# Attention as one pipeline of 48 head pairs, with two modulation units moved from VectorE to TensorE

## The chip, the cores and the metric

The kernel runs on one core of one Trainium2 chip. The metric is the device time of the whole program in microseconds (us); a comparison takes the medians of runs that alternate on the same chip.

## The reference, cut to what matters

Two layers of a diffusion backbone run over 512 latent tokens and 256 context tokens, with 1024 features. Every layer first turns a conditioning vector into six modulation vectors (shift, scale and gate for the mixer, shift, scale and gate for the feed-forward network), once for the latent stream and once for the context stream. Layer 0 mixes tokens by attention, layer 1 by retention; each is followed by a gated feed-forward network.

```python
mx = split(silu(c) @ ada_w[i] + ada_b[i], 6)          # latent; mc is the same with c_ctx
h_x = rms_norm(x, norm1_g) * (1 + mx[1]) + mx[0]
# layer 0: 16 heads of 64, 4 key/value heads, blocks of 128 queries; q and k are normalised, q_x and k_x rotated
s = [q @ k_ctx, q @ k_window (masked outside |i-j| <= 128), sink]   # context queries: k_ctx and sink alone
p = softmax(s);  o = p[:, ctx] @ v_ctx + p[:, window] @ v_window
x = x + mx[2] * (o @ w_o)
x = x + mx[5] * swiglu(rms_norm(x, norm2_g) * (1 + mx[4]) + mx[3])
```

The change concerns layer 0 alone, from the attention blocks to the start of its feed-forward network.

## The kernel before, in words

Activations are kept transposed, features on the 128 partitions and tokens along the free axis. A float32 product is made of three products of rounded parts (`mm3`, L145-151): high times high, low times high, high times low. Weights arrive as 512 KB chunks on SyncE's DMA queue (`w_raw`, L121); ScalarE rounds a chunk to its high part and VectorE subtracts to get the low part (`next_w`, L137).

**Order of work.** Apart from short stretches that are fixed by hand, a list scheduler places the instructions of every engine when the program is built. It goes by the order in which the Python code issues them, by when it thinks that operands are ready, and by which tile buffers are free. Each engine then runs its own list strictly in order, and waits at an instruction until the semaphores it needs have come.

**One block.** `Block` (L650) holds one group of four query heads, one stream and one block of 128 queries. There are 4 groups with 4 latent and 2 context blocks each, so 24 blocks, or 48 pairs of heads. For each head `score` (L660) issues the score products on TensorE into one of three PSUM banks (`S`, L685) and the masked minimum on VectorE (L686, a custom instruction that also stores the scores as the tile `pr`). After each second head it issues ScalarE's exponentials with row sums (L102, called through `lnexp`), VectorE's reciprocal (L696) and GpSimd's scaling of the two heads' probabilities (L699). `pr` has 8 buffers, so four pairs. `turn` (L701) transposes four 128x128 pieces of probabilities on TensorE into one of two PSUM banks `pT` (L705), and ScalarE or VectorE copies the bank to a tile `tt` (L709). `output` (L725) multiplies values by the transposed probabilities (L732) into `pO`.

**The loop.** `attend` (L749) takes one block after the other: the four heads' scores, then an optional filling piece, then all transposes of the block, then its output. After blocks 1 and 3 of groups 0 to 2 all four pieces of the next query tile's projection (`make_q`, L548) are issued in a row, between two blocks. During group 3 parts of the output projection (`out_part`, L833) are the filling pieces.

**Modulation.** In layer 0 the shift and the scale for the feed-forward network (parts 3 and 4 of `mods`) come from two places. Features 0 to 511 are made on TensorE before attention, in units of four feature tiles (`ada_unit`, L303; `UNITS` on L28 names the units made there, of which 8 and 6 are these). Features 512 to 1023 are made on VectorE during the rest of the output projection: `ada_tile` (L264) loads a 512 KB transposed tile on SyncE's queue and makes two multiply-and-sum instructions (L272), one for each stream; `cond_rows` (L256) loads the two conditioning vectors, spread over all partitions, and ScalarE applies the silu to them. `WO_ADA` (L30) says after which output tile how many of the eight tiles are issued.

**After attention.** The remaining output tiles follow in `WO_ORDER`. Each ends in a gated addition (L254), a square on ScalarE (L208 or L210) and an addition to the sum of squares (L211). After the tile (1, 4) the latent norm is closed (`rms`, L218 and L197 to L199). `latent_shape` (L909) then makes the eight operands of the feed-forward network, each by a scaling (L914), a rounding (L915) and a subtraction (L916), and `first_two` uses them one feature tile at a time.

Of the kernel before, what the change touches and what calls it, by code (L numbers as in the profile page):

```python
# [14 lines left out]
P = 128  # L15
# [6 lines left out]
NKV = 4  # L22
# [7 lines left out]
WO_ADA = {(0, 3): 1, (0, 4): 2, (0, 5): 2, (0, 6): 2, (0, 7): 1}  # L30
SPLIT_AT = (2, 4)
# [19 lines left out]
def dit_kernel(ctx, tc, xT, cT, crow, small, consts, masks, tabs0, tabs1, jtab, adaQ, adaN, adaT, wst, out):  # L51
# [132 lines left out]
    def t_sq(n):  # L184
        return T(rp, 512, "sq", 2)[:, :n]
# [464 lines left out]
    class Block:  # L650
# [9 lines left out]
        def score(self, i):  # L660
# [19 lines left out]
            for c0, w, m0, parts in runs:  # L680
                bank = pS()[:, :w]
                for p0, pw, kk in parts:
                    for r in range(2):
                        keys = kk[g][r] if kk is kc else kk[g][r][:, x0:x0 + pw]
                        nc.tensor.matmul(bank[:, p0:p0 + pw], qt, keys, start=r == 0, stop=r == 1)  # L685
                nc.vector.tensor_tensor_reduce(pt[:, c0:c0 + w], bank, mask[:, m0:m0 + w], 1.0, top, add, ALU.min, lo)  # L686
                top = lo
# [13 lines left out]
        def turn(self, kis, heads, eng):  # L701

            tp = pT()
            for i, (ki, hd) in enumerate((ki, hd) for ki in kis for hd in heads):
                nc.tensor.transpose(tp[:, i * P:(i + 1) * P], self.pr[hd][:, ki * P:(ki + 1) * P], ident)  # L705
# [3 lines left out]
            self.last = nc.scalar.copy(dst, tp) if eng == 0 else nc.vector.tensor_copy(dst, tp)  # L709
# [38 lines left out]

    def attend(g, s, b, *fills):  # L749
        blk = Block(g, s, b)  # L750
        for i in range(4):
            blk.score(i)
        for f in fills[:1]:
            f()
        blk.turns()
        for f in fills[1:]:
            f()
        blk.output()
# [57 lines left out]
    streams = ((0, xr), (1, cres))  # L816
# [13 lines left out]
    wo = [cut(next_w(ap, 1)), cut(next_w(ap, 1)), key_room_w(), cut(next_w(ap, 1))]  # L830
    begun = {}
# [13 lines left out]
    early = [(0, 0, 0, 3), (0, 0, 3, 6), (1, 0, 0, KT), (1, 1, 0, KT), (1, 2, 0, KT), (0, 1, 0, 6)]  # L845
    for (s, b), part in zip(context + latent, early):
        fills = [lambda: out_part(*part)]
        if (s, b) == latent[-1]:
            fills.append(lambda: out_part(1, 3, 0, KT, pS))
        attend(NKV - 1, s, b, *fills)  # L850
# [22 lines left out]
    assert not ada_wo  # L873
# [965 lines left out]
```

## Time and profile before

| | |
|---|---|
| median of 3 runs | 1772.69 us (1772.52 to 1777.53) |
| the profiled execution, whole | 1774.28 us |
| its span, first to last instruction | 1772.5 us |
| granted TensorE clock, mean | 0.995 |
| TensorE busy | 1716.1 us |
| VectorE, ScalarE, GpSimd busy | 1351.8, 845.4, 125.9 us |

Times in the profile are counted from the first instruction. The attention blocks run from about 104 to 331 us, the rest of the output projection from there to about 380 us, and the feed-forward network of layer 0 follows. PE is TensorE, PEld its weight loads, which run beside its products; DVE is VectorE, ACT ScalarE, POOL GpSimd, SP SyncE. An idle time is put down to the instruction whose end released the waiting one. A product is drawn longer than the interval at which the next one can start, so the busy time of PE hides short gaps.

### The profile page before, as it was taken

The page shows a single profiled execution, that of the slowest core. Times are in us where ns is not written, and L with a number is a line of the kernel's source. Part 1 is how long each engine was busy: PE and PEld are TensorE (multiplying, and loading weights), DVE is VectorE, ACT ScalarE, POOL GpSimd, SP SyncE. Part 2 cuts the span into 40 slices and gives each one's busy share as a digit, 9 for nine tenths or more (in the row PEclk, how much of TensorE's full clock was granted, in tenths as well). Part 3 has the DMA queues.
Part 4 walks back from the last instruction along what each step waited for, and adds up shares of the span by engine and source line. Part 5 has one row for each costly group of instructions (what it writes and reads, how often), then busy time and mean ns, then how long its engine had stood idle before and what let it go on. Part 6 is the DMA issues. An engine that isn't in the chain of part 4 may idle for free.

```text
span 1772.5 us, 27621 instructions
## 1 busy us (share of the span) xinstructions
PE 1716.1 (97%) x10852; PEld 1528.1 (86%) x10852; DVE 1351.8 (76%) x2366; ACT 845.4 (48%) x1486; POOL 125.9 (7%) x267
## 2 busy tenths in 40 slices
PE   6899999999999999999998999999999999999999
PEld 4787777779999999999977888898897899999998
DVE  6687777598778788777799858758768798777774
ACT  5476677455333334342465534524525564445442
POOL 0024334100000000000010000000000000000000
PEclk9999999999999999999999999999999999999999
DMA  8601012334243434343343434434433323233222
GB/s 337 238 25 37 25 43 66 118 123 152 83 144 119 156 107 154 112 152 110 116 133 104 160 97 140 151 102 132 155 96 119 95 77 116 94 109 107 96 84 84
DMA packets 59890, 206.68 MB, mean 117 GB/s; under 512 B 6640, under 2 KB 7024, under 8 KB 59504
## 3 DMA queue, kind: packets, MB, share of 16 engines
q1 hardware_dynamic: 52848, 179.75, 30.8%
q0 software_dynamic: 6912, 25.17, 4.5%
q8 instruction: 85, 1.39, 0.3%
q14 instruction: 45, 0.37, 0.1%
HBM read 202.80 MB, written 2.10 MB: 116 GB/s over the span
## 4 chain that ended last, share of the span: by engine, by line
PE 75%; DVE 14%; DMA 4%; ACT 3%; issue 2%; POOL 2%; SPq 0%; DVEq 0%; ACTq 0%; POOLq 0%
PE Y L883 14%; PE Z L883 7%; PE pj L149 6%; PE pj L151 6%; PE pj L150 6%; PE X L883 3%; PE Z L1241 3%; PE Y L1228 3%; DMA wraw<-in_wst_dram 3%; DVE wlo L167 3%; PE pT L705 2%; PE pO L732 2%; PE pj L1241 1%; PE X L1228 1%; POOL pr L699 1%
## 5 line engine op out<-in xcount | busy, mean ns | idle before, releaser
L166 ACT CAST whi<-wraw 128x1024 fp32r<-128x1024 f32 x177 | 185.8, 1053 | 307.2 <-PE Z L151 71.5
L167 DVE TENSOR_TENSOR wlo<-wraw,whi 128x1024 fp32r<-128x1024 f32 x177 | 216.0, 1223 | 42.3 <-ACT whi L166 41.9
L883 PE MATMUL Y<-aq,whi 128*128 128x384 f32 x640 | 173.5, 335 | 0.7 <-ACT hn L1021 0.7
L254 DVE SCALAR_TENSOR_TENSOR res<-pj,mod,res 128x512 f32<-128x512 f32 (+1 forms) x110 | 80.4, 731 | 68.4 <-PE pj L151 67.4
L142 DVE TENSOR_TENSOR wlo<-wraw,whi 128x1024 fp32r<-128x1024 f32 x79 | 96.5, 1223 | 35.3 <-ACT whi L141 34.3
L141 ACT CAST whi<-wraw 128x1024 fp32r<-128x1024 f32 x79 | 82.9, 1051 | 74.1 <-PE Z L151 24.2
L883 PEld LDWEIGHTS Y<-aq,whi 128*128 128x128 f32 x640 | 116.6, 188 | 1.7 <-ACT hn L1021 1.2
L883 PE MATMUL Y<-aq,wlo 128*128 128x384 f32 x320 | 107.0, 334 | 0.0
L272 DVE CUSTOM_DVE_ANT_0 y<-adaw,crow,small_sb 128x1024 bf16<-128x1024 f32 x64 | 81.9, 1280 | 31.6 <-DMA adaw<-in_adaT_dram 31.4
L102 ACT ACTIVATE pr<-pr,stat,qs 128x513 f32<-128x513 f32 (+2 forms) x96 | 74.4, 779 | 16.7 <-DVE stat L692 16.6
L1241 PE MATMUL Z<-whi,sA 128*128 128x512 f32 x256 | 81.0, 392 | 0.7 <-ACT whi L166 0.7
L699 POOL TENSOR_SCALAR pr<-pr,stat 128x512 f32<-128x512 f32 (+2 forms) x96 | 69.1, 733 | 90.6 <-DVE stat L696 86.4
L149 PE MATMUL pj<-ax,whi 128*128 128x512 f32 x176 | 68.7, 391 | 0.0
L151 PE MATMUL pj<-ax,whi 128*128 128x512 f32 x176 | 68.7, 390 | 0.0
L150 PE MATMUL pj<-ax,wlo 128*128 128x512 f32 x176 | 68.5, 389 | 0.0
L705 PE MATMUL pT<-const_sb,pr 128*128 128x128 f32 x352 | 58.0, 283 | 9.8 <-POOL pr L699 7.8
L149 PE MATMUL pj<-act,whi 128*128 128x512 f32 x168 | 66.0, 393 | 0.0
L150 PE MATMUL pj<-act,wlo 128*128 128x512 f32 x168 | 65.9, 392 | 0.0
L151 PE MATMUL pj<-act,whi 128*128 128x512 f32 x168 | 65.5, 390 | 0.0
L705 PEld LDWEIGHTS pT<-const_sb,pr 128*128 128x128 f32 x352 | 39.3, 140 | 27.9 <-POOL pr L699 21.0
L269 POOL DMA_DIRECT2D adaw<-in_adaT_dram x48 | 25.7, 535 | 516.9 <-DVE mod L272 419.8
L686 DVE CUSTOM_DVE_ANT_0 pr<-S,mask,qs 128x256 f32<-128x256 f32 (+1 forms) x96 | 52.6, 566 | 10.9 <-PE S L685 9.2
(539 smaller groups left out, 5275.2 us busy)
## 6 DMA issues: line engine op xcount, KB each, us to landing
wraw<-in_wst_dram SPq DMA_DIRECT2D x238, 512.0 KB, 3.7
adaw<-in_adaT_dram POOLq DMA_DIRECT2D x48, 512.0 KB, 3.9
wx<-in_wst_dram SPq DMA_DIRECT2D x24, 512.0 KB, 4.7
adan<-in_adaQ_dram SPq DMA_DIRECT2D x16, 512.0 KB, 7.8
adan<-in_adaN_dram SPq DMA_DIRECT2D x16, 512.0 KB, 8.8
res<-in_xT_dram SPq DMA_DIRECT2D x16, 256.0 KB, 4.2
adaw<-in_adaT_dram SPq DMA_DIRECT2D x8, 512.0 KB, 4.0
aq<-in_adaN_dram SPq DMA_DIRECT2D x12, 256.0 KB, 5.6
```

The costliest lines, as they stand in the source:

```text
L141: nc.scalar.copy(hi, raw)
L142: nc.vector.tensor_tensor(lo, raw, hi, op=sub)
L149: nc.tensor.matmul(o, whi, xhi, start=first, stop=False)
L150: nc.tensor.matmul(o, wlo, xhi, start=False, stop=False)
L151: return nc.tensor.matmul(o, whi, xlo, start=False, stop=last)
L166: nc.scalar.copy(hi, t)
L167: return nc.vector.tensor_tensor(lo, t, hi, op=sub)
L272: after(nc.vector.tensor_tensor_reduce(junk, w, cr[:, s * 1024:(s + 1) * 1024], 1.0, sm_t[:, C_ADAB + l * 48 + j:C_ADAB + l * 48 + j + 1], ...
L699: nc.gpsimd.tensor_scalar(pt[:, :n], pt[:, :n], st[:, 6 + e:7 + e], 1.0, op0=mult, op1=mult)
L705: nc.tensor.transpose(tp[:, i * P:(i + 1) * P], self.pr[hd][:, ki * P:(ki + 1) * P], ident)
L883: nc.tensor.matmul(o, p, r, start=first and k + i == 0, stop=k == 3 and i == 2, skip_group_check=not first)
L1241: ins = nc.tensor.matmul(o, p, r, start=first and k + i == 0, stop=k == 3 and i == 2, skip_group_check=not first)
```

## The change

1. `attend` is gone. One loop runs over the 48 head pairs. In step `i` it issues the scores of pair `i`, then the transposes of pair `i - 2` (`LAG`), then filling pieces listed by step number (`steps`), then the output of a block whose second pair has been transposed. The first transpose in a step is ordered behind the last score product of the step's first head (`behind`).
2. The four pieces of each query projection are issued in different steps.
3. The eight feature tiles of parts 3 and 4 no longer run on VectorE. Units 7 and 9 make them on TensorE in group 3, each in two halves over the contraction (`unit_half`): four loads of 256 KB into buffers of the query tiles, 16 small products, a copy by ScalarE, a transpose, two small additions by VectorE. `cond_rows`, the eight 512 KB loads and the 16 VectorE instructions before the feed-forward network go.
4. Splitting of outputs, stream loads and output weights are placed at steps too.

What follows the output projection is not changed; it stands 25 lines further down.

```diff
-WO_ADA = {(0, 3): 1, (0, 4): 2, (0, 5): 2, (0, 6): 2, (0, 7): 1}
-SPLIT_AT = (2, 4)
+LAG = 2
...
-        def turn(self, kis, heads, eng):
+        def turn(self, kis, heads, eng, behind=()):
...
+                if i == 0:
+                    after(ins, behind)
...
-        def turns(self):
+        def turns(self, p, behind):
             n = len(self.keys)
-            for p in range(2):
-                for ki in range(0, n - 1, 2):
-                    self.turn((ki, ki + 1), (2 * p, 2 * p + 1), ki // 2 % 2)
-            if n % 2:
+            for ki in range(0, n - 1, 2):
+                self.turn((ki, ki + 1), (2 * p, 2 * p + 1), ki // 2 % 2, () if ki else behind)
+            if p and n % 2:
                 self.turn((n - 1,), (0, 1, 2, 3), 0)
...
-    for g in range(NKV - 1):
-        for i, (s, b) in enumerate(latent + context):
-            attend(g, s, b)
-            if i in (1, 3):
-                for piece in make_q(2 * g + 2 + i // 3):
-                    piece()
-            if (g, i) == SPLIT_AT:
-                split_o(0)
-                split_o(1)
-    split_o(2)
-    xr = load_stream(0)
-    cres = load_stream(1)
...
-    early = [(0, 0, 0, 3), (0, 0, 3, 6), (1, 0, 0, KT), (1, 1, 0, KT), (1, 2, 0, KT), (0, 1, 0, 6)]
-    for (s, b), part in zip(context + latent, early):
-        fills = [lambda: out_part(*part)]
...
-        attend(NKV - 1, s, b, *fills)
+    def unit_half(u, c):
+
+        part, o, w = u // 2, pT()[:, 0:P], []
+        for k in range(4 * c, 4 * c + 4):
+            w.append(T(ap, 512, "q", 9))
+            nc.sync.dma_start(w[-1], adaN[u, k // 2][:, k % 2 * 512:k % 2 * 512 + 512])
+        for k in range(4):
+            for j in range(4):
+                nc.tensor.matmul(o[32 * j:32 * j + 32, :], ccol[:, 4 * c + k, :], w[k][:, j * P:(j + 1) * P],
+                                 start=k == 0, stop=k == 3)
+        rows = t_sq(P)
+        nc.scalar.copy(rows, o)
+
+        def finish():
+            t = pT()[:, 0:P]
+            nc.tensor.transpose(t, rows, ident)
+            tv = t.rearrange("p (j c) -> p c j", c=32)
+            for s in range(2):
+                col = mods[0, s][:, part, 4:8]
+                nc.vector.tensor_tensor(col, tv[:, s, :], col if c else sm_t[:, C_ADAB + 4 * u:C_ADAB + 4 * u + 4], op=add)
...
+    for g in range(NKV - 1):
+        a, b = make_q(2 * g + 2), make_q(2 * g + 3)
+        for r, fs in ((0, a[0:1]), (2, a[1:2]), (3, a[2:4]), (5, b[0:1]), (8, b[1:2]), (9, b[2:3]), (10, b[3:4])):
+            steps[12 * g + r] = list(fs)
+    steps[34].append(lambda: split_o(0))
+    steps[35] = [lambda: split_o(1), weight]
+    last = {1: [lambda: unit_half(7, 0)], 2: [lambda: split_o(2), load_streams, lambda: out_part(0, 0, 0, 4), end],
+            3: [lambda: unit_half(7, 1), weight], 4: [lambda: out_part(0, 0, 4, 6), end],
+            5: [lambda: unit_half(9, 0), lambda: weight(key_room_w)], 6: [end, lambda: out_part(1, 0, 0, KT)],
+            7: [lambda: unit_half(9, 1), weight], 8: [end, lambda: out_part(1, 1, 0, KT)],
+            10: [lambda: out_part(1, 2, 0, KT)], 11: [lambda: out_part(0, 1, 0, 3)],
+            12: [lambda: out_part(0, 1, 3, 6)], 13: [lambda: out_part(1, 3, 0, KT, pS)]}
+    steps.update({12 * (NKV - 1) + r: fs for r, fs in last.items()})
+    blocks = [Block(g, s, b) for g in range(NKV) for s, b in (latent + context if g < NKV - 1 else context + latent)]
+    for i in range(2 * len(blocks) + LAG):
+        behind = ()
+        if i < 2 * len(blocks):
+            blk = blocks[i // 2]
+            blk.score(i % 2 * 2)
+            behind = [blk.scored]
+            blk.score(i % 2 * 2 + 1)
+        j = i - LAG
+        if j >= 0:
+            blk = blocks[j // 2]
+            blk.turns(j % 2, behind)
+        for f in steps.get(i, ()):
+            f()
+        if j >= 0 and j % 2:
+            blk.output()
...
-    ada_wo = [(part, d) for part in (3, 4) for d in range(4, KT)]
...
-    cr = cond_rows(wo_p)
+    (_, xr), (_, cres) = streams
     for s, d in WO_ORDER:
-        ins = out_part(s, d, 0, KT)
-        for _ in range(WO_ADA.get((s, d), 0)):
-            ada_tile(0, *ada_wo.pop(0), (0, 1), cr, [ins], wo_p)
+        out_part(s, d, 0, KT)
         if (s, d) == (1, 4):
             ln_exp_turn()
             rms(0)
```

More of the change, by code (lines that the diff above doesn't have):

```diff
@@ L684, in score @@
                         keys = kk[g][r] if kk is kc else kk[g][r][:, x0:x0 + pw]
-                        nc.tensor.matmul(bank[:, p0:p0 + pw], qt, keys, start=r == 0, stop=r == 1)
+                        self.scored = nc.tensor.matmul(bank[:, p0:p0 + pw], qt, keys, start=r == 0, stop=r == 1)
                 nc.vector.tensor_tensor_reduce(pt[:, c0:c0 + w], bank, mask[:, m0:m0 + w], 1.0, top, add, ALU.min, lo)
@@ L699, in score @@
                 nc.gpsimd.tensor_scalar(pt[:, :n], pt[:, :n], st[:, 6 + e:7 + e], 1.0, op0=mult, op1=mult)
-        def turn(self, kis, heads, eng):
+        def turn(self, kis, heads, eng, behind=()):
             tp = pT()
             for i, (ki, hd) in enumerate((ki, hd) for ki in kis for hd in heads):
-                nc.tensor.transpose(tp[:, i * P:(i + 1) * P], self.pr[hd][:, ki * P:(ki + 1) * P], ident)
+                ins = nc.tensor.transpose(tp[:, i * P:(i + 1) * P], self.pr[hd][:, ki * P:(ki + 1) * P], ident)
+                if i == 0:
+                    after(ins, behind)
             while len(self.tt) <= kis[0] // 2:
@@ L747, in output @@
             nc.vector.tensor_copy(dst, O.rearrange("p (e q) -> p e q", e=2))
[L749 to L758, printed above, removed]
     def split_o(g):
@@ L803, in dit_kernel, with load_streams @@
     latent, context = ([(s, b) for b in range(n)] for s, n in ((0, 4), (1, 2)))
[L804 to L816 removed]
+    streams = []
+    def load_streams():
+        streams.extend(((0, load_stream(0)), (1, load_stream(1))))
     def cut(w):
@@ L843, in out_part @@
         return ins
-    early = [(0, 0, 0, 3), (0, 0, 3, 6), (1, 0, 0, KT), (1, 1, 0, KT), (1, 2, 0, KT), (0, 1, 0, 6)]
-    for (s, b), part in zip(context + latent, early):
-        fills = [lambda: out_part(*part)]
-        if (s, b) == latent[-1]:
-            fills.append(lambda: out_part(1, 3, 0, KT, pS))
-        attend(NKV - 1, s, b, *fills)
+    def unit_half(u, c):
[16 more added lines that the diff above has]
+                nc.vector.tensor_tensor(col, tv[:, s, :], col if c else sm_t[:, C_ADAB + 4 * u:C_ADAB + 4 * u + 4], op=add)
+        ends.append(finish)
@@ new lines, in dit_kernel @@
+    ends = []
+    end = lambda: ends.pop(0)()
+    weight = lambda room=None: wo.append(room() if room else cut(next_w(ap, 1)))
+    steps = {}
+    for g in range(NKV - 1):
[10 more added lines that the diff above has]
+            12: [lambda: out_part(0, 1, 3, 6)], 13: [lambda: out_part(1, 3, 0, KT, pS)]}
@@ L872, in dit_kernel @@
             rms(0)
-    assert not ada_wo
     A.close()
```

3 lines of the change are left out of this document (1 added, 2 removed).

## The prediction

> **What bounds the kernel now.** I read the page first: the busy times, and the chain that ended last.
>
> ```profile
> span 1772.5 us, 27621 instructions
> ...
> PE 1716.1 (97%) x10852; PEld 1528.1 (86%) x10852; DVE 1351.8 (76%) x2366; ACT 845.4 (48%) x1486; POOL 125.9 (7%) x267
> ...
> PE 75%; DVE 14%; DMA 4%; ACT 3%; issue 2%; POOL 2%; SPq 0%; DVEq 0%; ACTq 0%; POOLq 0%
> ```
>
> TensorE is the bound, so what the change is worth is what it takes out of TensorE's waits, less what it adds to TensorE's work. Next come the windows of the two stages that it touches: attention, and the change-over from the output projection to the feed-forward network.
>
> ```profile
> core 0: us, PE busy (x) PEld busy (x) DVE busy (x) ACT busy (x) POOL busy (x), PEclk, DMA share, GB/s
> 103.80:330.70 226.90, 216.85 (x1519) 172.06 (x1518) 169.41 (x546) 154.87 (x368) 86.38 (x190) 1.00 0.11 34
> ...
> 369.00:380.00 11.00, 10.18 (x78) 8.96 (x77) 11.00 (x22) 4.80 (x9) 0.00 (x0) 1.00 0.18 48
> 380.00:390.00 10.00, 6.82 (x27) 4.17 (x27) 10.00 (x18) 9.93 (x18) 0.00 (x0) 1.00 0.28 106
> 390.00:420.00 30.00, 30.00 (x204) 29.70 (x206) 27.49 (x51) 19.52 (x39) 0.39 (x1) 1.00 0.55 188
> ```
>
> In attention PE seems 96% busy and VectorE is at 169.41 of 226.90 us, 75%: no helper is full. From 369 to 390 VectorE is busy without a pause, and PE lacks 0.82 + 3.18 = 4.0 us. After 390 PE is full, and in the built order of the changed kernel all that follows the change-over stands as before (8070 TensorE instructions, unbroken to the end). So a microsecond won before 390 is won at the end. The granted clock (PEclk) is 1.00 throughout and gives nothing.
>
> A product is drawn longer than its interval, so I look at the weight loads' waits in the attention window for the true gaps, and at one gap in the timeline.
>
> ```profile
> PEld pT L705 <- POOL pr L699: 21.0, 48, 1.3
> PEld S L685 <- DVE stat L686: 2.3, 8, 0.5
> PEld pO L732 <- ACT tt L709: 1.8, 6, 0.5
> ```
> ```profile
> 143.82 0.30 PE L705 MATMUL pT<-const_sb,pr 128*128 128x128 f32 x1
> 144.88 0.33 PE L705 MATMUL pT<-const_sb,pr 128*128 128x128 f32 x1 [0.77 <-POOL pr L699]
> ```
>
> Transposes wait 48 times, 21.0 us together, for GpSimd's scaled probabilities; all else is small. This is what the lag aims at.
>
> **The lag.** How long does TensorE have between the last score product of a pair and its first transpose, and how long do the probabilities take? The first comes from the built orders of both kernels, counting the products that stand between, each at its interval.
>
> ```profile
> 344.70 0.39 PE L150 MATMUL pj<-h,wlo 128*128 128x512 f32 x1
> 344.93 0.39 PE L151 MATMUL pj<-h,whi 128*128 128x512 f32 x1
> ...
> 297.40 1.95 PE L732 MATMUL pO<-tt,v 128*64 128x256 f32 x16
> ...
> 301.51 1.04 PE L705 MATMUL pT<-const_sb,pr 128*128 128x128 f32 x8
> ```
>
> 512 columns start 0.23 us apart, so 384 and 256 columns cost 0.17 and 0.115; eight transposes take 1.04 us, of which the last is drawn at 0.28, so 0.11 each; a value product is 0.11 likewise. On this scale the 48 pairs of the kernel before have a median of 5.0 us of TensorE work between their last score and their first transpose. In the changed order it is 7.0 us. For the second number I follow the last two pairs from their score products to GpSimd:
>
> ```profile
> 313.19 0.40 PE L685 MATMUL S<-k,q 128*128 128x256 f32 x2
> ...
> 316.74 0.49 PE L685 MATMUL S<-k,q 128*128 128x256 f32 x2
> ```
> ```profile
> 319.56 1.36 POOL L699 TENSOR_SCALAR pr<-pr,stat 128x512 f32<-128x512 f32 x2 [4.51 <-DVE stat L696]
> 321.16 1.37 POOL L699 TENSOR_SCALAR pr<-pr,stat 128x512 f32<-128x512 f32 x2 [0.24 <-DVE stat L696]
> ```
>
> Scores end at 313.59, the first head is scaled at 319.56 + 0.68 = 320.24: 6.6 us. For the other pair, 317.23 to 321.85: 4.6 us. Summing over the pairs what is missing to such a time: at 4.6 us the old order lacks 8.2 us and the new one 1.1; at 6.6 us the old lacks 63.7 and the new 23.4. The measured wait of 21.0 lies between, since one wait also gives the pairs behind it their time. A time of 5.2 us reproduces it (old 20.8), and then the new order lacks 4.4. Scaling the 6.6 us case to the measured wait instead, 23.4 x 21.0 / 63.7 = 7.7 remain. I take 7, near the less favourable end, because the helpers' same work then falls into less time. **The lag brings 21.0 - 7 = 14 us**, with bounds of 0 (the chain gets as much later as the transposes do) and 21.
>
> The query pieces are the same instructions, spread; they cost nothing themselves and are part of the counted distances. With lag 2, three pairs of `pr` are live and there is room for four, so GpSimd's small copies into a new `pr` need not wait for transposes of a pair that is late; were they to wait, the scaling queued behind them on GpSimd would wait as well, which is within the bound of 0.
>
> **Off VectorE.** Sixteen instructions leave the output projection.
>
> ```profile
> L272 DVE CUSTOM_DVE_ANT_0 junk<-adaw,crow,small_sb x16: 1273/1278/1286, 348.3 to 373.9; 128x1024 bf16<-128x1024 f32 x16
> ```
> ```profile
> 375.05 0.69 DVE L199 SCALAR_TENSOR_TENSOR y<-sq,y 128x512 f32<-128x512 f32 x1
> ...
> 378.07 0.74 DVE L914 SCALAR_TENSOR_TENSOR act<-res,acol,y 128x512 f32<-128x512 f32 x1
> ```
> ```profile
> 371.75 0.64 ACT L197 ACTIVATE sq<-y 128x512 f32<-128x512 f32 x1
> ```
> ```profile
> 380.86 0.44 PE L149 MATMUL Y<-aq,whi 128*128 128x384 f32 x1 [0.72 <-ACT whi L141]
> ...
> 384.26 0.44 PE L149 MATMUL X<-aq,whi 128*128 128x384 f32 x1 [0.69 <-ACT aq L915]
> ```
>
> They are 16 x 1.28 = 20.5 us of VectorE, but not of the path: from 331 to 369 PE runs on. What they delay is the norm. ScalarE has its square at 372.39, VectorE finishes the norm only at 375.74 and starts the first operand at 378.07. Without them I count from 372.4: the two steps of the norm, L198 and L199, at 0.69 each give 373.8; what the changed order puts between them and the first operand (a gated addition and sums of squares, half as wide) may take as much again, 375.2. So the first operand starts 3 to 4 us sooner. PE lacks 4.0 us there, and the chain of eight operands behind the first is as long as before, with context squares and a weight split between its links, so some of the waits on ScalarE and VectorE stay. I take **3 us**, with 1 and 4 as bounds. The weights move up past eight 512 KB loads and the 1 MB row on SyncE's queue; PE did not wait for them there, so that earns nothing.
>
> **On to TensorE.** Units 7 and 9 add 64 small products and 4 transposes.
>
> ```profile
> L309 PE MATMUL pj<-aq,ccol x96: 272/273/297, 419.1 to 421.6; 128*32 128x128 f32 x96
> ```
>
> 2.5 us for 95 steps are 0.026 us each, so 64 x 0.026 + 4 x 0.11 = 2.1 us, and about 1 us for going to and fro between other products: **3 us**. ScalarE's four copies and VectorE's eight small additions are no more than what fills their idle quarter. The loads are the less certain part.
>
> ```profile
> aq<-in_adaN_dram SPq DMA_DIRECT2D x12, 256.0 KB, 5.6
> ...
> crow<-in_adaN_dram SPq DMA_DIRECT2D x4, 256.0 KB, 4.1
> ```
>
> Their buffers come from the nine of the query tiles, of which six are live in group 3. So the fourth load of the first half waits on SyncE until TensorE has read a context query for the last time; behind it in the queue stand stream loads that wait for `split_o(2)`, then the next half's loads, then output weights. Between that release and the product that needs the fourth load, the order has 3.3 us of TensorE work; a group of four takes 4.1 us to land, so about 0.8 is missing. I put 0.5 on each of four halves: **2 us**, with 0 and 4 x 5.6 = 22 as bounds. A half also keeps one of the two `pT` banks; that is in the 2.
>
> The Trainium skill's "DMA: Bandwidth & Descriptors" (Anatomy of one DMA) gives a load a fixed cost of about 2.0 us plus its bytes at 436 GB/s, so a 256 KB load would be an estimated 2.6 us, and the fourth load would then arrive before it is needed. The rows of this trace, 4.1 and 5.6 us for loads issued in groups, do not agree with that as a price here; by the page the sum would be 2 us lower.
>
> **The sum.** -14 - 3 + 3 + 2 = -12 us, against the profiled execution's 1774.28 (span 1772.5 and 1.8 around it): 1762.3. The median of the runs, 1772.69, is 1.6 below the profiled time, so I forecast 1772.7 - 12 = **1760.7 us**.
>
> **Rivals.**
> (a) The chain is the limit, not its start: probabilities come later as the transposes do, because VectorE, ScalarE and GpSimd work their own lists in order. Then the lag brings perhaps 4 us and the sum is -4 - 3 + 3 + 2 = -2: **1770.7**. For it: ends of 6.6 us above bare work. Against it: VectorE at 75%, ScalarE at 154.87 of 226.90.
> (b) Loads of the unit halves come late, slower than before: TensorE's list is in order, so each half can hold it for a whole landing, 4 x 5.6 = 22.4 us. -14 - 3 + 3 + 22.4 = +8.4: **1781**. It turns the sign once a half costs over 14 / 4 = 3.5 us. For it: the queue behind `split_o(2)` and the buffers released late. Against it: 3.3 us of work ahead of the first of them, and DMA at 11% in this window. At the page's 2.6 us a half, this rival would end at about 1769, no slower than before.
> (c) All waits go, in both stages: -21 - 4 + 3 + 0 = -22: **1750.7**.
> (d) The scheduler undoes the order, so nothing moves: **1772.7**. The built order speaks against it (5.0 against 7.0 us).
>
> **How the numbers follow.** Forecast 0.62, its own range 1753 to 1768; (a) 0.14; (b) 0.10; (c) 0.10; (d) 0.04. A difference under 0.3% (5.3 us) can't be told from none. Faster: 0.61 of the forecast, (c), and 0.03 of (a): 0.74. Same: the rest of (a), (d) and the forecast: 0.16. Slower: 0.10. The range from (c) to just beyond (a) and (d), 1750 to 1774, leaves out (b) and the far end of (c), about 0.2 at most.
>
> **What would show it.** Right: the wait of the transposes for L698 (now L699) near 7 us; the first operand (L939) 3 us sooner after the norm's square, with PE's idle time there down to about 1 us; waits of PE for `adaN` loads in group 3 near 2 us. Wrong: transposes waiting 15 us or more although they stand later (a); one of the unit products waiting 3 us and more for a load (b); or new waits of scores for their bank (2.3 us now) or of value products for copies (1.8 us now) that take the place of the old one.

## The result, and the profile after

The changed kernel takes 1767.7 us against 1773.0 for the one before, medians of nine alternating runs each. The ratio of their means is 0.9967 (95% interval 0.9956 to 0.9977), so 5.9 us faster (4.1 to 7.8); the medians alone differ by 5.3. The forecast was 12 us. The direction held, and half of the gain is missing.

The page of the changed kernel (its profiled execution took 1765.14 us, the one of before 1774.28, so this pair is 9.1 us apart, more than the means):

```profile
span 1763.4 us, 27889 instructions
...
PE 1716.5 (97%) x10984; PEld 1531.5 (87%) x10984; DVE 1332.7 (76%) x2342; ACT 841.3 (48%) x1487; POOL 122.4 (7%) x267
```

The windows of the same stages as in the prediction (length, busy time of TensorE, its weight loads, VectorE, ScalarE and GpSimd, granted clock, DMA share, GB/s):

```profile
103.20:325.70 222.50, 219.56 (x1651) 176.93 (x1650) 169.08 (x556) 155.19 (x372) 82.95 (x190) 0.99 0.17 53
...
364.00:374.00 10.00, 9.60 (x77) 8.85 (x76) 8.52 (x16) 7.34 (x13) 0.00 (x0) 1.00 0.34 104
374.00:385.00 11.00, 9.10 (x46) 7.47 (x46) 9.84 (x17) 10.18 (x18) 0.00 (x0) 1.00 0.37 117
385.00:415.00 30.00, 30.00 (x281) 29.55 (x280) 28.76 (x55) 19.96 (x43) 0.75 (x1) 1.00 0.59 196
```

And TensorE's waits in attention, by what ended them (total us, times, longest):

```profile
PEld pT L704 <- issue: 6.2, 17, 0.4
PEld S L684 <- DVE stat L685: 4.7, 11, 1.4
PEld pT L704 <- POOL pr L698: 3.9, 10, 0.7
...
PEld pT L832 <- issue: 1.4, 5, 0.4
```

The transposes' wait for GpSimd fell from 21.0 us to 3.9, more than was forecast. Yet attention, from the start of its first score product to the start of its last value product, only went from 226.6 us (103.8 to 330.4) to 222.1 (103.2 to 325.3). The stretch from there to the first product of the feed-forward network, and from that to the end of its first part (the `crow` products), went from 49.2 to 48.5 and from 42.9 to 40.5. So the change-over gave the 3 us that were forecast. Attention gave 4.5 us, where the sum had 9. Two things in these rows were not in that sum: scores wait up to 1.4 us at once for VectorE, where before the longest was 0.5, and the granted clock of the stage is 0.99.

Short windows at the start of attention show where both sit. The changed kernel:

```profile
110.00:115.00 5.00, 4.43 (x33) 4.07 (x31) 4.88 (x15) 4.79 (x10) 1.03 (x7) 1.00 0.22 89
115.00:120.00 5.00, 3.77 (x23) 3.13 (x24) 5.00 (x17) 4.94 (x11) 2.45 (x4) 0.95 0.32 101
120.00:125.00 5.00, 5.00 (x26) 4.54 (x25) 2.97 (x9) 2.46 (x8) 2.53 (x6) 0.71 0.02 7
125.00:130.00 5.00, 5.00 (x35) 3.50 (x34) 4.80 (x15) 3.44 (x7) 0.14 (x2) 1.00 0.00 0
```

TensorE rests 0.57 + 1.23 = 1.80 us between 110 and 120 while VectorE is full, and behind that rest the clock is 0.95 and then 0.71: 5 x (0.05 + 0.29) = 1.7 us of work lost. VectorE's timeline tells what it was full with:

```profile
115.34 0.61 DVE L685 CUSTOM_DVE_ANT_0 pr<-S,mask,stat 128x384 f32<-128x384 f32 x1
...
115.94 1.23 DVE L141 TENSOR_TENSOR wlo<-wraw,whi 128x1024 fp32r<-128x1024 f32 x1
117.09 0.60 DVE L685 CUSTOM_DVE_ANT_0 pr<-S,mask,stat 128x384 f32<-128x384 f32 x1
```
```profile
117.76 0.50 PE L684 MATMUL S<-kc,q 128*128 128x256 f32 x2 [1.13 <-DVE stat L685]
```

Between two masked minima stands the subtraction that splits a query weight, and the next score product waits 1.13 us for its bank behind it. VectorE had no room for it: the prediction went by 75% over the whole stage, but in the kernel before VectorE (the third busy time) was already full near the stage's start:

```profile
105.00:110.00 5.00, 5.00 (x29) 4.30 (x28) 4.93 (x16) 4.92 (x12) 0.48 (x4) 1.00 0.00 0
110.00:115.00 5.00, 4.91 (x35) 4.43 (x33) 4.88 (x13) 3.71 (x7) 2.65 (x6) 1.00 0.00 0
```

The changed kernel has such splits at 107.3 and 115.9; in the kernel before, the first two of attention stand at 133.0 and 136.2. The reason is in the diff: `make_q` splits its weight when it is called, and the new table `steps` calls it for all six remaining query tiles before the loop starts. Program order is a list scheduler's priority, so the splits went as far forward as their buffers allowed.

### The profile page after: what moved, and what is told of

Its sections match the earlier page's. It is cut to its first block, busy times and chain, and to the rows that moved or that the text cites. A ratio compares the mean times of both kernels' runs of the same rounds, so it can differ in the third digit from the quotient of the medians.

```text
span 1763.4 us, 27889 instructions
## 1 busy us (share of the span) xinstructions
PE 1716.5 (97%) x10984; PEld 1531.5 (87%) x10984; DVE 1332.7 (76%) x2342; ACT 841.3 (48%) x1487; POOL 122.4 (7%) x267
## 4 chain that ended last, share of the span: by engine, by line
PE 78%; DVE 12%; DMA 5%; ACT 3%; issue 1%; POOL 0%; SPq 0%; DVEq 0%; ACTq 0%; POOLq 0%
PE Y L908 14%; PE Z L908 7%; PE pj L150 7%; PE pj L149 7%; PE pj L148 7%; DMA wraw<-in_wst_dram 4%; PE X L908 3%; PE Y L1253 3%; PE Z L1266 3%; DVE wlo L166 3%; PE pO L732 2%; PE pT L704 2%; PE S L684 2%; PE pj L1266 2%; PE X L1253 1%
## 5 line engine op out<-in xcount | busy, mean ns | idle before, releaser
L698 POOL TENSOR_SCALAR pr<-pr,stat 128x512 f32<-128x512 f32 (+2 forms) x96 | 65.3, 693 | 76.6 <-DVE stat L695 57.7
L908 PE MATMUL Y<-sA,whi 128*128 128x256 f32 x304 | 60.8, 282 | 0.0
L908 PEld LDWEIGHTS Y<-aq,wlo 128*128 128x128 f32 x320 | 60.1, 188 | 0.0
```

What stands on the lines that cost most here:

```text
L908: nc.tensor.matmul(o, p, r, start=first and k + i == 0, stop=k == 3 and i == 2, skip_group_check=not first)
```

## The experiments

All ratios below are to the kernel before on the same chip, and "us" is what the ratio lacks to 1, times its median there (1776.7, 1773.7 and 1775.1 us in the three groups). Attention is measured as above, in the one profiled execution that each kernel has. "At full clock" takes off what the 5 us windows of the stage show as clock below 1.00. Behind the last `crow` product all fourteen kernels run the same list of instructions on TensorE, VectorE and ScalarE, and yet that stretch takes between 1349.1 and 1354.6 us in their profiled executions. So a whole time moves by a few us that no edit made, and where a whole time and a stage differ, the argument goes by the stage.

**The parts by themselves: the lag without the units, the units elsewhere, no units, lag 3.** For the lag alone, `unit_half` and its ends leave the steps and VectorE's sums return:

```diff
+WO_ADA = {(0, 3): 1, (0, 4): 2, (0, 5): 2, (0, 6): 2, (0, 7): 1}
-    last = {1: [lambda: unit_half(7, 0)], 2: [..., lambda: out_part(0, 0, 0, 4), end],
+    last = {2: [..., lambda: out_part(0, 0, 0, 4)],
...
     for s, d in WO_ORDER:
-        out_part(s, d, 0, KT)
+        ins = out_part(s, d, 0, KT)
+        for _ in range(WO_ADA.get((s, d), 0)):
+            ada_tile(0, *ada_wo.pop(0), (0, 1), cr, [ins], wo_p)
```

> The pipeline with lag 2 and the spread query pieces, but the modulation of features 512 to 1023 back on VectorE in the rest of the output projection, as before. From the last score of a pair to its first transpose the built order now has a median of 6.5 us of TensorE work (7.0 with the units in between, 5.0 before), so some 2 us of the transposes' wait come back. Theory U (the units cost 7.5 us where they sit among the score and value products, not 5): the attention stage, 222.1 us in the changed kernel, falls by 7.5 - 2 to about 216.5 and the change-over is about 3 us longer again: 1767.7 - 5.5 + 3.2 = 1765.4 us, about 7.5 below before. Theory L (the lag itself brings little, because score products now wait for VectorE, and the units cost the 5 that were forecast): attention about 219, whole time 1768 us, 5 below before. If the units were as good as free, attention would stay at 222 or rise, and the time be 1771.

0.9938 (0.9926 to 0.9951), 11.0 us faster; attention 213.8 us (103.5 to 317.2), no clock lost. So the lag with the spread pieces takes 12.8 us off attention, and of the 21.0 us of waits this is left:

```profile
PEld pT L705 <- POOL pr L699: 5.7, 14, 0.7
PEld pT L705 <- issue: 5.0, 13, 0.4
PEld S L685 <- DVE stat L686: 3.7, 7, 1.4
```

The changed kernel's attention is 222.1 - 1.7 = 220.4 at full clock, so its units cost 6.6 us there: more than the 5 forecast and more than the 3.2 that they save. Theory L, that the lag itself brings little, falls; theory U holds in the stages. The whole time came out 3.5 us lower than U gave; of that, attention is 2.7 us shorter than its 216.5.

Whole units between output tiles, after the tiles (0, 4) and (0, 6):

```diff
+        if (s, d) in UNIT_AT:
+            u = UNIT_AT[s, d]
+            fin[u] = ada_unit(u, uw[u])
```

> Lag 2, and units 7 and 9 on TensorE, but whole and between output tiles of the rest of the output projection, where all products have 512 columns and no bank of the transposes is in demand. Attention must be that of the kernel with the lag alone (U: 216.5; L: 219). The units' own work is 128 records x 0.026 = 3.4 us and two transposes; theory U says that the rest of the 7.5 (switching among short products, the bank held) is due to the place and falls away here: output projection up to the first operand longer by 4, change-over as short as in the changed kernel: 1765.4 - 3.2 + 4 = 1766. If the 7.5 belong to the units wherever they are, 1769.7. If L holds with units at 4, 1769.

0.9946 (0.9933 to 0.996), 9.6 us faster. Attention at full clock is 213.6, that of the lag alone; the rest of the output projection is 52.9 instead of 48.5 us, so there the units cost 4.4, against 6.6 in attention. Place matters, as U said, but 4.4 is still more than the 3.2 saved, and the time cannot be told from that of the lag alone.

Neither units nor sums; the modulation of features 512 to 1023 is left out, and its tiles hold the bias alone:

```diff
+    for part in (3, 4):
+        for s in range(2):
+            nc.vector.tensor_copy(mods[0, s][:, part, 4:8], sm_t[:, C_ADAB + 8 * part + 4:C_ADAB + 8 * part + 8])
```

> Lag 2 with neither the units nor VectorE's sums: the modulation of features 512 to 1023 is left out (its tiles hold the bias alone). The price of both places is read against this kernel. Theory U: attention 216.5, first operand as early after the last tile as in the changed kernel, 1767.7 - 5.5 = 1762 us. Theory L: 219 and 1764.7. The kernel with the lag alone must lie about 3.2 above it (change-over), the kernel with the units later about 4 above it.

0.9933 (0.992 to 0.9945), 11.9 us faster. The change-over (40.5 us against 43.2 with VectorE's sums) is shorter as forecast, but the median lies only 1 us below that of the lag alone. For the profiled pair the trace has the answer: in this execution the windows from 115 to 125 have clocks of 0.78 and 0.54, 3.4 us lost, and in that of the lag alone none. At full clock both have the same attention, 213.9 and 213.8.

The changed kernel with lag 3:

```diff
-LAG = 2
+LAG = 3
...
-    steps.update({12 * (NKV - 1) + r: fs for r, fs in last.items()})
+    steps.update({12 * (NKV - 1) + r + 1: fs for r, fs in last.items()})
```

> The changed kernel with lag 3, so that a pair is transposed three pairs after its scores; the steps of group 3 stand one step later. The built order has a median of 10.1 us of TensorE work between (7.0 with lag 2), more than any chain from scores to scaled probabilities that the traces showed (4.6 to 6.6). Now four pairs of probabilities are live and there are four pairs of buffers, so a new pair's buffer comes free only with the transposes just before. If the rest of the transposes' wait (3.9 us for GpSimd) is all that is left of the lag's account: it goes, 1767.7 - 4 = 1764 us. If GpSimd's small copies into a new buffer now wait for the transposes, and scores with them through VectorE, new waits of scores for their bank take its place: equal or slower, 1768 to 1780. Where the lag never was the point (L), no change: 1767 to 1769.

0.9941 (0.9927 to 0.9954), 10.5 us faster, so 4.6 below the changed kernel, near the 4 of the first theory. But attention only fell from 220.4 to 219.2 at full clock: the wait for GpSimd is down to 2.1 us, and that of scores for VectorE is 4.9 where it was 4.7. As profiled the stage is no shorter at all (222.6), so where the 4.6 us lie is not shown.

**The dose of the lag, the spreading, and the units in the old loop.** Three kernels have the lag alone (VectorE's sums) with lag 1, with lag 2 and query pieces in one step, and with lag 3; one is the kernel before with the units alone.

Lag 1; one filling piece at the end of group 3 moves a step forward with it:

```diff
-LAG = 2
+LAG = 1
...
```

> The kernel with the lag alone (VectorE's sums as before), but lag 1: pairs are transposed one step after their scores; the loop, the spread query pieces and all else stay. Counted as in the prediction, the built order has a median of 5.1 us of TensorE work from a pair's last score to its first transpose, against 5.0 before and 6.5 with lag 2; for a chain of 5.2 us that lacks 21.2 us in sum, against 20.8 before. Theory D (the distance alone decides): the transposes' wait for GpSimd is back at about 20 us and the time at that of before, 0 to 3 us below it. Theory S (the gain comes from the loop with spread pieces, whatever the lag): it stays 11 us below before.

0.9987 (0.9977 to 0.9998), 2.3 us faster, as theory D said, but not for its reason. Attention at full clock is 220.4, so 6.2 us shorter than before, and the wait is

```profile
PEld pT L705 <- POOL pr L699: 11.9, 33, 1.0
PEld S L685 <- DVE stat L686: 5.5, 10, 1.4
```

11.9 us where the count of distances gave 21.2. The count overrates the waits of the new loop. What keeps the whole time near that of before is in part the start of attention: TensorE rests 1.80 us between 115 and 120, and 1.7 us of clock are lost behind the rest.

Lag 2, the four query pieces in one step:

```diff
-        for r, fs in ((0, a[0:1]), (2, a[1:2]), (3, a[2:4]), (5, b[0:1]), (8, b[1:2]), (9, b[2:3]), (10, b[3:4])):
+        for r, fs in ((3, a), (7, b)):
```

> The kernel with the lag alone, lag 2, but the four pieces of each query projection issued in one step again (steps 3 and 7 of each group, as the loop before had them). Median distance 6.1 us, but uneven: pairs with no projection between have little, and for a chain of 5.2 us the sum of what is missing is 19.3 us (6.6 with spread pieces, 20.8 before). Theory D: the wait stays near 20 us and most of the gain is lost, 0 to 4 us below before. If the spreading brings nothing and the lag all: 11 below before, as with spread pieces.

0.9963 (0.9948 to 0.9978), 6.6 us faster. At full clock attention is 215.5, only 1.7 above that with spread pieces, and the wait for GpSimd is 5.7 us, the same. Theory D's count is wrong again (19.3). Spreading the pieces is worth little by itself. The profiled execution also lost 3.4 us of clock (0.99, 0.50, 0.83 from 115 to 130), and the two together would be about the 4.4 us between this kernel and the lag alone; but it was the longest of its six runs, and whether the others lost as much is not known.

The kernel before with the units alone:

```diff
+    halves = [(7, 0), (7, 1), (9, 0), (9, 1)]
...
+        fills = [lambda: [out_part(*part)] + [end() for _ in ends[:1]]]
+        if halves:
+            fills.append(lambda: unit_half(*halves.pop(0)))
```

> The kernel before with the third part of the change alone: the four unit halves are filling pieces of group 3 in the old loop, behind a block's transposes, their ends with the next block's filling piece; VectorE's 16 sums go. If the units cost what they cost in the changed kernel, 6.8 us at the clock of 1.00, and the change-over gains 3.2, the time is 3.6 us above before. If the 3 us that they cost beyond their own 3.85 us of work come from the pipeline (banks and waits that the old loop does not have), 0.6 above. If their work lies in the old loop's waits, which it puts off, 1 to 3 below before.

1.0024 (1.0015 to 1.0033), 4.3 us slower. Attention is 233.4, which is 6.8 more than before, at full clock in both; the change-over gains what it gains in the changed kernel. Beside the 3.2 us that it saves, this part of the change is a loss wherever it stands in attention: it costs 6.8 in the old loop, 6.6 with lag 2, 7.8 with lag 3 (219.2 less the 211.4 of the next run).

> The kernel with the lag alone, with lag 3. Median distance 9.2 us; for a chain of 5.2 us only 1.0 us is missing in sum (6.6 with lag 2). Theory D by itself: the 5.7 us of waits for GpSimd go, 16 us below before. But with the units in it, lag 3 took 1.3 us off attention at equal clock: the waits of score products for VectorE and for their order grew by about as much as the transposes' waits fell. If that holds here, 12 us below before, and the bound has moved from the transposes' operand to the scores' banks.

The edit is that of lag 3 above. 0.9938 (0.9926 to 0.995), 11.0 us faster. At full clock attention is 211.4, 2.4 below lag 2, and the wait for GpSimd is 1.6 us; but the execution lost 3.4 us of clock at 115 to 125, so as profiled the stage is no shorter (214.8 against 213.8), and the whole gains are alike.

**The split of the query weights.** The table now calls `make_q` at steps, three ahead of the first piece; nothing else changes. Once in the kernel with lag 3 and VectorE's sums, once in the changed kernel:

```diff
-        a, b = make_q(2 * g + 2), make_q(2 * g + 3)
-        for r, fs in ((0, a[0:1]), (2, a[1:2]), (3, a[2:4]), (5, b[0:1]), (8, b[1:2]), (9, b[2:3]), (10, b[3:4])):
-            steps[12 * g + r] = list(fs)
+        for j, made, at in ((2 * g + 2, 12 * g - 3, (0, 2, 3, 3)), (2 * g + 3, 12 * g + 2, (5, 8, 9, 10))):
+            steps.setdefault(made, []).append(lambda j=j: pieces.update({j: make_q(j)}))
+            for n, r in enumerate(at):
+                steps.setdefault(12 * g + r, []).append(lambda j=j, n=n: pieces[j][n]())
+    steps.pop(-3)[0]()
```

> Lag 3 without units, and the query weights split as late as in the loop before: the table of steps no longer builds all query pieces ahead of the loop, so the roundings and subtractions of the next weights (L142, 1.2 us of VectorE each) leave the first blocks, where VectorE has no pause. In every lagged kernel so far but the one with the lag alone, TensorE rests 1.2 to 1.8 us between 112 and 119 us, because score products wait for VectorE, and in the 5 to 10 us behind that rest the granted clock is 0.54 to 0.95. Theory P (the rest at the start and the clock behind it are part of what the prediction lacks): the rest shrinks by about 1.1 us, the clock there stays at 1.00, attention (214.8 as profiled, 211.4 at a full clock) comes to 210 to 212 as profiled and the time to 14 us below before. Rival (VectorE is full there with other work, the split only moves): a rest of the same size a few us later, and 11 below before.

0.9904 (0.9891 to 0.9916), 17.0 us faster, 6 more than with the early split, more than the 14 of theory P, and better than both kernels of the case. (The kernel with the lag alone, which the expectation leaves out, rests 1.8 us there too; what it lacks is the lower clock.)

> The same single edit in the changed kernel itself (lag 2, units in group 3). Theory P: attention 222.1 as profiled comes to about 219.5, the time from 5.8 to about 9 us below before. Rival: no change, 6 below.

0.9934 (0.9921 to 0.9947), 11.7 us faster: twice the gain of the changed kernel, and close to what was forecast for it. Its windows, to be held against those shown above:

```profile
110.00:115.00 5.00, 4.90 (x39) 4.60 (x38) 4.92 (x17) 3.72 (x9) 1.35 (x2) 1.00 0.00 0
115.00:120.00 5.00, 5.00 (x35) 4.56 (x35) 4.64 (x14) 4.59 (x11) 2.41 (x5) 1.00 0.01 3
120.00:125.00 5.00, 4.98 (x34) 3.23 (x32) 4.85 (x12) 3.15 (x7) 2.00 (x4) 1.00 0.00 0
125.00:130.00 5.00, 4.87 (x33) 4.19 (x32) 5.00 (x19) 2.03 (x6) 1.59 (x2) 1.00 0.34 105
```

The rest of 1.80 us is down to 0.10, VectorE is as full as before, the clock stays at 1.00, and the next split stands at 125.2. Scores now wait 2.6 us for VectorE instead of 4.7, at most 0.6 at once. Attention is 218.2 us: 3.9 less than in the changed kernel, of which 1.7 is clock. With lag 3 it is 207.9 against 214.8, of which 3.4 is clock. Theory P holds in both, and the rival falls: the next split, at 125.2, costs TensorE a rest of only 0.13 us in its window. The edit moves a weight's load and ScalarE's rounding along with the split. The load runs from 125 to 130 now, at 105 GB/s and with neither rest nor dip, so it was not the load; that it was VectorE's subtraction is read from the row at 115.94. The start of attention comes 0.8 us sooner as well. Together that is 4.7 of the 5.8 us between the two kernels' gains; where the rest lies is not shown.

**What the units cost, and VectorE's copies.** A quarter of the units' products; three of the four steps of each sum are left out, so the columns are partial sums:

```diff
-        for k in range(4):
+        for k in range(3, 4):
...
-                                 start=k == 0, stop=k == 3)
+                                 start=True, stop=True)
```

> The changed kernel with a quarter of the units' products: of the four steps of each half over the contraction only the last is made (its modulation columns are partial sums), 32 records instead of 128; loads, copies, transposes, banks and places stay. If the units' 6.8 us were all in the products, attention falls by 5.1; if beyond the products' issue time (0.0265 us a record) nothing depends on their number, by 96 x 0.0265 = 2.5, from 220.5 at a full clock to 218; if the price is the banks and the waits around them, by less than 1. Whole time about 8 below before in the middle case.

0.9953 (0.9941 to 0.9965), 8.3 us faster, the middle case. Attention at full clock is 217.5 (220.9 less 3.4 of clock), 2.9 below the changed kernel for 96 records less: 0.030 us a record, near the issue interval. At that rate all 128 records are worth 3.9 of the 6.6 us. With a quarter of them the units still cost 3.7 us, so some 2.7 us do not go with the number of products (up to 1.0 of them are waits for loads, shown further down).

Lag 3 without units, all copies on ScalarE:

```diff
-                self.turn((ki, ki + 1), (2 * p, 2 * p + 1), ki // 2 % 2, () if ki else behind)
+                self.turn((ki, ki + 1), (2 * p, 2 * p + 1), 0, () if ki else behind)
```

> Lag 3 without units, all copies of transposed probabilities on ScalarE (VectorE had one in three). With lag 3 the transposes' wait for GpSimd is down to 1.6 us and the largest waits are those of score products: 3.5 us for VectorE's minimum and 5.8 as issue. If VectorE is now the limit of attention, taking some 20 us of copies off it removes those 3.5 us and the pause at the start: 14 below before. If ScalarE's copies come late instead (value products then wait for L711), no change or a loss: 8 to 11 below before.

0.9934 (0.9921 to 0.9947) against 0.9938 with lag 3 and shared copies: no difference. Attention at full clock is 212.2 against 211.4, and scores wait for VectorE longer, not less:

```profile
PEld S L685 <- DVE stat L686: 6.0, 12, 1.5
```

So VectorE's mean load was not the limit. The one wait of 1.5 us is still there, and so are the early splits.

Attention in the traces, us:

| kernel | as profiled | lost to the clock | at full clock |
|---|---|---|---|
| before | 226.6 | 0 | 226.6 |
| changed | 222.1 | 1.7 | 220.4 |
| changed, late split | 218.2 | 0 | 218.2 |
| changed, lag 3 | 222.6 | 3.4 | 219.2 |
| changed, a quarter of the units | 220.9 | 3.4 | 217.5 |
| units alone | 233.4 | 0 | 233.4 |
| lag 1, no units | 222.1 | 1.7 | 220.4 |
| lag 2, no units | 213.8 | 0 | 213.8 |
| lag 2, units later | 215.4 | 1.7 | 213.6 |
| lag 2, neither units nor sums | 217.3 | 3.4 | 213.9 |
| lag 2, no units, pieces in one step | 218.9 | 3.4 | 215.5 |
| lag 3, no units | 214.8 | 3.4 | 211.4 |
| lag 3, no units, copies on ScalarE | 212.2 | 0 | 212.2 |
| lag 3, no units, late split | 207.9 | 0 | 207.9 |

Three rows bear out the taking-off: lag 2 without units, with the units later, and with neither. Their attention is the same list of instructions on TensorE, VectorE and ScalarE, and it took 213.8, 215.4 and 217.3 us with 0, 1.7 and 3.4 us lost. So in this stage a lost us of clock is a lost us of time, and whether none, one or two such losses come is not set by the list. It is no rule for the whole kernel: behind the last `crow` product the kernel before loses 8.5 us of clock and the changed one 1.7, and the stretch takes 1350.0 and 1349.1 us.

## Why the prediction was right or wrong

**The lag, -14: right in size, and partly by luck.** Attention fell by 12.8 us with the lag alone, and the wait for GpSimd in the changed kernel is 3.9 us where 7 was taken. The bound of 0 and rival (a) fall: the chain did not get later as the transposes did. But the count of distances behind the 7 does not hold. It gave 21.2 us for lag 1 and 19.3 for pieces in one step, where 11.9 and 5.7 were measured. With lag 1, whose counted distance is that of before (5.1 against 5.0), attention is already 6.2 us shorter; the second step of lag brings the other 6.6. So about half of the gain came with the new loop and not with the distance; through what, was not tried. Nor is it so that GpSimd's small copies into a new `pr` need not wait for transposes. They still wait, 35.9 us in 31 waits in the kernel before and 47.1 in 25 in the changed one:

```profile
POOL pr L668 <- PE pT L704: 47.1, 25, 4.5
```

That cost the transposes little, since their own wait for the scaling fell all the same.

**Off VectorE, -3: right.** The change-over gave 0.7 + 2.5 = 3.2 us. The norm's square ends at 367.50 and the first operand starts 2.0 us later, where it was 5.7 before:

```profile
366.87 0.63 ACT L196 ACTIVATE sq<-y 128x512 f32<-128x512 f32 x1
```
```profile
369.46 2.07 DVE L939 SCALAR_TENSOR_TENSOR act<-res,acol,y 128x512 f32<-128x512 f32 x3
```

That is 3.7 us sooner, within the 3 to 4 that were counted. TensorE's idle time there is 0.40 + 1.90 = 2.3 us, not the 1 that was named as a sign; operands still come late (`X` waits 1.2 us for `aq`).

**On to TensorE, +3 and +2: the sum was short by 1.6, and its split was wrong.** Units cost 6.6 us with lag 2. First, the number: the trace has two records for each of these products.

```profile
L832 PE MATMUL pT<-q,ccol x128: 272/273/297, 267.6 to 294.5; 128*32 128x128 f32 x128
...
  issue: 1.4, 5
  ACT tt L710: 0.2, 1
  PE pT L704: 0.2, 1
```

The 0.026 us were taken from a row of such records and multiplied by 64 instead of 128: 3.4 us, not 1.7. Second, the loads: no product of the units waited for one, which the three releasers above show, so that term was 0 instead of 2, and rival (b) with it (in the kernels with lag 3, with a quarter and with the late split one or two did wait for a load, for 0.3 to 1.0 us in all).

```profile
q<-in_adaN_dram SPq DMA_DIRECT2D x16, 256.0 KB, 3.2
```

They landed in 3.2 us. The Trainium skill's "DMA: Bandwidth & Descriptors" (Anatomy of one DMA) has its formula for loads issued by GpSimd; applied to these loads of SyncE it gave an estimated 2.6. The rows of the kernel before gave 4.1 and 5.6, and the 3.2 measured lies between, nearer to the page. Third, "about 1 us for going to and fro" was too little. Three of the four halves are no runs of 32 records, but cut up among other products, one of them in pieces of 8 (PEld rows are weight loads, with what ended the idle time before them):

```profile
281.84 0.43 PE L832 MATMUL pT<-q,ccol 128*32 128x128 f32 x8
282.38 0.30 PEld L684 LDWEIGHTS S<-k,q 128*128 128x128 f32 x2 [0.38 <-DVE stat L685]
282.38 0.62 PE L684 MATMUL S<-k,q 128*128 128x384 f32 x2
282.92 0.16 PEld L832 LDWEIGHTS pT<-q,ccol 128*32 128x32 f32 x8 [0.25 <-issue]
282.92 0.43 PE L832 MATMUL pT<-q,ccol 128*32 128x128 f32 x8
283.28 0.30 PEld L684 LDWEIGHTS S<-kc,q 128*128 128x128 f32 x2 [0.20 <-DVE stat L685]
283.28 0.51 PE L684 MATMUL S<-kc,q 128*128 128x256 f32 x2
...
283.62 0.34 PE L684 MATMUL S<-k,q 128*128 128x384 f32 x1
```

Eight records and two score products of 384 columns take 282.92 - 281.84 = 1.08 us, where 8 x 0.026 + 2 x 0.17 = 0.55 were their intervals; eight records and two products of 256 columns take 283.62 - 282.92 = 0.70 instead of 0.44. So 0.53 and 0.26 us are lost around these two pieces, in part because the score product waits for VectorE to free its bank (the 0.38 and 0.20). The 128 records stand in 11 pieces, so the 2.8 us beyond the work (6.6 less 3.4 and four transposes of 0.11) are 0.25 a piece. With a quarter of the products there are 5 pieces, and 3.7 - 32 x 0.026 - 4 x 0.11 = 2.4 us beyond the work. Of these, up to 1.0 are two waits for loads, which the changed kernel does not have:

```profile
  DMA q<-in_adaN_dram: 1.0, 2
```

The other 1.4 us are 0.28 a piece. The units later stand in two whole runs, and 4.4 - 3.4 - 2 x 0.11 = 0.8 us are left there, 0.4 a run. So this part of the price goes roughly with the number of pieces; that the changes make up all of it, and by what, was not tried by itself.

**The step that failed: "The query pieces are the same instructions, spread; they cost nothing themselves".** They are the same instructions, but building them for all groups ahead of the loop moved the splitting of their weights into the start of attention, which the built order of VectorE would have shown and of which the prediction only counted TensorE's. The moved splits let TensorE rest 1.8 us there, and in the profiled execution a lower clock follows. With them put back, the gain is 11.7 us against a forecast of 12: what the prediction put at nothing cost 5.8 us (11.7 less 5.9), 4.7 of them in and before attention. That these agree so well is partly luck. Attention is 8.4 us shorter then, where -14 + 3 + 2 = -9 was forecast, but if the units cost their 6.6 us there as well, the lag brings 15 and makes up for them. Of the signs named as wrong, "new waits of scores for their bank" was the one that came, 2.3 us to 4.7; it was no rival with a price.

The sum as measured, for the profiled pair: lag -12.8, units +6.6, clock +1.7, change-over -3.2, start of attention 0.6 sooner: -8.3, against spans that differ by 9.1; the stretch behind the last `crow` product, which the change leaves as it was, has another 0.9. The means differ by less, 5.9; the profiled execution of the changed kernel was the shortest of its runs.

## What to carry to other kernels

When a change only moves instructions, follow what else is issued with them: a closure that prepares its operands when it is made does that work where the table is built, and a list scheduler then puts it first. Read the built order of the helper engines as well as that of the bound one, above all where a helper has no idle time. And price work that goes to the bound engine by records rather than by instructions in the source, and by the pieces into which it is cut: here 3.2 us saved beside the path cost 6.6 on it, of which 3.8 are records and transposes.

## What the runs showed of the hardware

A short rest of TensorE can be followed by a lower clock that costs as much again, or twice that. All ten kernels with the early split rest 1.3 to 1.8 us between 110 and 120 us, and in eight of them the clock behind it is lower, by 1.7 us of work in three and by 3.4 in five, for instance (lag 3, no units):

```profile
110.00:115.00 5.00, 4.35 (x33) 4.01 (x31) 4.88 (x15) 4.93 (x10) 1.03 (x5) 1.00 0.17 66
115.00:120.00 5.00, 3.85 (x19) 3.26 (x18) 5.00 (x14) 4.94 (x12) 2.03 (x4) 0.69 0.36 108
120.00:125.00 5.00, 5.00 (x22) 4.53 (x21) 3.16 (x9) 2.89 (x9) 1.91 (x4) 0.63 0.00 0
```

The lag alone rests 1.8 us there as well and keeps 1.00, and so does the kernel with all copies on ScalarE; the kernel before rests 1.39 us at 120 to 125 and keeps it too. With the late split there is neither rest nor dip. So a lower clock often follows a rest of this size and does not always; with one profiled execution of each kernel, which rests are followed by one stays open. That the list of instructions does not decide it is shown by the three kernels with the same attention above, which have none, one and two losses of 1.7 us. The stretch itself, in the changed kernel and in the one with neither units nor sums, is at half clock:

```profile
119.50:122.90 3.40, 3.40 (x14) 3.21 (x13) 3.32 (x9) 2.25 (x8) 2.19 (x4) 0.50 0.14 53
```
```profile
117.90:124.50 6.60, 6.60 (x28) 6.21 (x28) 4.77 (x13) 3.62 (x10) 3.37 (x6) 0.50 0.23 78
```

The Trainium skill's "TensorE: Matmul & The Clock Gate" (What's actually happening) says that the clock halves after an idle window of about 3.4 us that runs freely, and comes back after a busy one. The two rows, half clock for 3.4 us and for 6.6, agree with one such window or two. That the dips here follow rests of 1.3 to 1.8 us, shorter than an idle window, does not agree with that section, and here the traces decide.
